# Seven-product pairs from feature tile 4 on: operands summed in place on VectorE, no negated operand, 57 activation slots

## The chip, the cores and the metric

The kernel runs on one core of one Trainium2 chip. The metric is device time of one launch in microseconds (us). TensorE (PE) does the matrix products, VectorE (DVE) and ScalarE (ACT) the elementwise work, GpSimd (POOL) a little elementwise work and the issue of those DMAs that add into their destination; SyncE (SP) issues the loads of weights.

## The reference

One step of a decoder trunk with one layer, in float32, for 520 tokens (512 prompt positions and 8 single-token samples), model width 1024, feed-forward width 3072:

```
x = x + W_o( sum_b sigmoid(g_b) * P_b(mixer_b(rmsnorm(x))) )    # pooling, RG-LRU and chunked gating branches
xn = rmsnorm(x, norm2_g)
g_pre = xn @ wg                                        # 1024 -> 3072
h = gelu(causal_conv3(prefix ++ g_pre)) * (xn @ wu)    # depthwise, width 3
x = x + h @ wd ;  y = rmsnorm(x, final_norm_g)
```

Beside `y`, the last rows of the inputs of each convolution, of the pooling window and of the recurrent state are returned. The change sits in the feed-forward part (`wg`, `wu`, `wd`) and in the loading of the old states and two small constants.

## The kernel before, in words

Activations lie transposed: features on the 128 partitions, the 520 tokens along the free axis, as two halves of 260. Every operand of a product is split into a high and a low part, and a product of a 128x128 weight tile with 520 tokens is three passes (high x high, high x low, low x high) over two halves, six matmuls of 260 columns (`mm`, line 202). A feature tile of `wg` or `wu` (m = 0 to 23) needs eight such k steps, 48 matmuls; this is the unit of time t in which the schedule counts.

**Order of the work.** The program has no scheduler behind it: each engine executes its instructions in the order in which the Python text issues them. `job` puts matrix products in a list; `run_jobs` (line 290) issues them and keeps a clock `now` that counts one unit per 48 matmuls. Work that belongs beside them is registered by `after(n, fn)` and `at(t, fn)` and issued when the clock passes that time (`run_later`, line 219); of equal times the one that was registered first goes first. So a step at t = 2.25 is placed behind everything that was issued before, on each engine, and an engine that waits for one instruction holds all later ones.

**Weights.** A `Chunk` is loaded by SP (`load`), rounded to its high part by ACT (`high`), and its low part is either a DVE subtraction (`low`, line 127) or, with `by_dma`, a negated copy on ACT and a DMA issued by POOL that adds the original weight from memory (`low_by_dma`, line 97). There are 4 raw, 6 high and 6 low buffers.

**Feed-forward.** After the eighth `w_o` product (t = 0 in this text) `g_post` and `fg_post` (lines 830, 936) take the `wg` products, `fg_rest` (842) does the convolution: one ACT pass (`tap0`), two DVE passes and a short one (`taps`), the gelu on ACT, and for m < 4 a DVE multiplication with the row factor of the norm (`scaled`). `u2_post` (951) multiplies with the `wu` product; `later_hilo` (964) splits the result for `wd`. The norm factor itself is computed by `rstd_small` (446) at the end of tile 0 and spread over the partitions by `rstd_bcast` (490) at the end of tile 1.

Tiles m = 0 to 3 use the unnormalized x times gain. Tiles 4 and 5 use normalized operands (`plain`, 897). From m = 6 on (`MP = 6`, line 1151) two feature tiles form a `Pair` (133): both tiles, as a 2x2 block matrix by k halves and tile, against the activations as a 2x2 block matrix by k halves and token halves, are computed with seven block products instead of eight (`PRODUCTS`, 143), 84 matmuls instead of 96. Sums of weight blocks are made by `sums` (172), split by `high` and `low`. The activation side needs seven operands X0 to X6, each as high and low part, made once by `operands` (915) from normalized blocks b (`rows`, 874), with DVE sums (`diff`) and splits (`operand`, 880). `run_pair` (244) issues a pair in the order of `SEQ_PAIR` (1150), 2.75 units long, with two `wd` products as fillers between the seven products:

```
SEQ_PAIR = (0, (0, 0), 3, 2, (0, 1), 1, 4, 5, (1, 0), 6, (1, 1))
```

Product 0 takes the weight operand h1, product 3 h2, product 2 h3; the low part of h3 is issued a quarter unit after the pair's start (`steps`, 189). X0 is a negated copy of X8, made on POOL (`minus_first`, 907). All activations come from one group of `NA = 51` equal slots (`A`, line 63).

Of the kernel before, what the change touches and what calls it, by code (L numbers as in the profile page):

```python
# [16 lines left out]
P = 128  # L17
# [34 lines left out]
def trunk_kernel(ctx: ExitStack, tc: tile.TileContext, t: dict, o: dict):  # L52
# [35 lines left out]
    sts = const.tile([P, NSTATE], F32, name="sts")  # L88
    wsT = const.tile([P, 4, P], F32, name="wsT")
    bsb = const.tile([P, 4, P], F32, name="bsb")  # L90
# [11 lines left out]
    class Chunk:  # L102
# [30 lines left out]
    class Pair:  # L133
# [29 lines left out]
        def low1(self):  # L163
            v.tensor_sub(self.new("h1", "wl"), self.raw[1], f(self.W["h1", "wh"]))  # L164
# [125 lines left out]
    def run_jobs():  # L290
# [3 lines left out]
        for n, e in enumerate(jobs):  # L294
            if e is None:
# [3 lines left out]
                for dt, fn in ((-2.25, c.load), (-0.75, c.high), (-0.5, c.low)):  # L299
                    at(t1 + dt, fn)  # L300
# [83 lines left out]
    def constants():  # L384
        nc.sync.dma_start(sts, t["sts"])
        nc.sync.dma_start(wsT, t["wsT"])
        nc.sync.dma_start(bsb.rearrange("p g i -> p (g i)"), t["bs"].partition_broadcast(P))
# [248 lines left out]
    def pool_post(gi, ps):  # L636
# [9 lines left out]
        def sums():  # L646
            g.tensor_copy(views["pool"][:, gi, :], a[:, SEQ:])
            v.tensor_reduce(st, pls[:, gi, :, 16 - w:], axis=mybir.AxisListType.X, op=ALU.add)
# [100 lines left out]
    def vmix(k):  # L749
        ps = PS1("vm")  # L750
        for c in range(4):
            te.matmul(ps[:, c * P:(c + 1) * P], vtok[c][:, k * P:(k + 1) * P], wsT[:, k, :], start=True, stop=True)  # L752
        m = A(f"mix{k}")
        v.tensor_tensor(m[:, :SEQ].rearrange("p (c i) -> p c i", c=4), ps.rearrange("p (c i) -> p c i", c=4),
                        bsb[:, k:k + 1, :].to_broadcast([P, 4, P]), op=ALU.add)
# [59 lines left out]
    def wo_post(j, ps):  # L815
# [3 lines left out]
        st2[0] = square_add(st2[0], x1[j], f"x1q{j}")  # L819

# [9 lines left out]
    def fg_post(m, ps):  # L830
# [5 lines left out]
        if m < MN:  # L836
            v.tensor_mul(two(ext[:, 2:]), acc(ps), two(rs2[0]))
        else:
            s.activation(two(ext[:, 2:]), acc(ps), AF.Copy)
        fg_rest(m, ext)  # L840

    def fg_rest(m, ext):
        y = A(f"fc{m}")

        def tap0():
            v.tensor_copy(views["ff"][:, m, :], ext[:, SEQ:])
# [9 lines left out]
        def scaled():  # L856
            if m < MN:
# [12 lines left out]
    def half_rows(q):  # L870
        i, h = q
        bq[q] = [A(f"b{i}{h}_{n}") for n in range(2)]

# [6 lines left out]
    def operand(n, xs):  # L880
        xo[n] = [(A(f"X{n}{i}h", F32R), A(f"X{n}{i}l", F32R)) for i in range(2)]
        for x, (h, _) in zip(xs, xo[n]):
            s.activation(h, x, AF.Copy)

        def lows():
            for x, (h, l) in zip(xs, xo[n]):
                v.tensor_sub(l, x, f(h))

        after(0.3, lows)
# [7 lines left out]
    def plain(k):  # L897

        return [[two(xo[n][k % 4 // 2][e])[:, k % 2, :] for n in ((8, 7), (1, 5))[k // 4]] for e in range(2)]

    def diff(n, a, b):
        y = [A(f"d{n}{i}") for i in range(2)]
        for i in range(2):
            v.tensor_sub(y[i], a[i], b[i])
        return y

    def minus_first(i):
        hl = [A(f"X0{i}_{e}", F32R) for e in "hl"]
        for q, p in zip(hl, xo[8][i]):
            g.tensor_scalar(q, f(p), -1.0, None, op0=ALU.mult)  # L910
        xo.setdefault(0, []).append(hl)

    dd = {}
# [336 lines left out]
```

## Time and profile before

| | |
|---|---|
| time, median of 3 runs | 870.24 us (870.08 to 870.30) |
| the profiled execution | 870.54 us, of which the span of the trace is 868.5 us |
| PE busy | 857.8 us (99%) in 7144 matmuls |
| DVE busy | 590.5 us (68%) |
| ACT busy | 443.4 us (51%) |
| POOL busy | 128.9 us (15%) |
| PE's time waiting for others | 3.8 us, in five waits |

The span runs from the first to the last instruction; 2.04 us of the execution lie around it. An engine's busy time counts overlapped work once. The start of an instruction minus the start of the one before it on the same engine is what one costs in an unbroken sequence; it is shorter than the duration given, since consecutive instructions overlap a little.

### The profile page before, as it was taken

The page shows a single profiled execution, that of the slowest core. Times are in us where ns is not written, and L with a number is a line of the kernel's source. Part 1 is how long each engine was busy: PE and PEld are TensorE (multiplying, and loading weights), DVE is VectorE, ACT ScalarE, POOL GpSimd, SP SyncE. Part 2 cuts the span into 40 slices and gives each one's busy share as a digit, 9 for nine tenths or more (in the row PEclk, how much of TensorE's full clock was granted, in tenths as well). Part 3 has the DMA queues.
Part 4 walks back from the last instruction along what each step waited for, and adds up shares of the span by engine and source line. Part 5 has one row for each costly group of instructions (what it writes and reads, how often), then busy time and mean ns, then how long its engine had stood idle before and what let it go on. Part 6 is the DMA issues. An engine that isn't in the chain of part 4 may idle for free.

```text
span 868.5 us, 16891 instructions
## 1 busy us (share of the span) xinstructions
PE 857.8 (99%) x7144; PEld 853.7 (98%) x7144; DVE 590.5 (68%) x920; ACT 443.4 (51%) x649; POOL 128.9 (15%) x185
## 2 busy tenths in 40 slices
PE   9999999999999999999999999999999999999996
PEld 7999999999999999999999999999999999999995
DVE  5897989698774443235554787677777767768655
ACT  6655465478342343222336675556556556556542
POOL 0502411111100000020002114111111110111143
PEclk9999999999999999999999999999999999999997
DMA  8433233222223233343345975655546555555642
GB/s 281 140 116 121 67 106 91 73 93 87 84 80 116 73 98 122 98 150 96 118 137 161 217 159 120 159 125 130 151 110 158 130 110 154 134 127 151 148 102 99
DMA packets 36251, 108.40 MB, mean 125 GB/s; under 512 B 4152, under 2 KB 7352, under 8 KB 36152
## 3 DMA queue, kind: packets, MB, share of 16 engines
q1 hardware_dynamic: 25440, 83.08, 30.4%
q0 software_dynamic: 9216, 22.68, 14.0%
q10 hardware_dynamic: 1520, 1.57, 0.5%
q8 instruction: 56, 0.92, 0.5%
q14 instruction: 19, 0.16, 0.1%
HBM read 92.13 MB, written 15.57 MB: 124 GB/s over the span
## 4 chain that ended last, share of the span: by engine, by line
PE 97%; DVE 1%; DMA 1%; ACT 0%; issue 0%; POOL 0%; DVEq 0%; POOLq 0%; ACTq 0%
PE pj L206 73%; PE pa L257 12%; PE c L257 6%; PE pf L257 3%; PE lru L206 1%; DMA x<-in_x 1%; PE vm L752 0%; DMA par<-in_par 0%; PE po L206 0%; DVE bc L522 0%; DVE y L1069 0%; PE vt L745 0%; ACT L540 0%; PE n30p L452 0%; PE n31p L452 0%
## 5 line engine op out<-in xcount | busy, mean ns | idle before, releaser
L127 DVE TENSOR_TENSOR wl<-raw,wh 128x1024 fp32r<-128x1024 f32 (+1 forms) x108 | 126.3, 1175 | 36.6 <-ACT wh L118 36.5
L206 PE MATMUL pj<-xn_h,wh 128*128 128x260 f32 x704 | 141.9, 283 | 0.1
L206 PE MATMUL pj<-xn_l,wh 128*128 128x260 f32 x704 | 141.4, 282 | 0.0
L206 PE MATMUL pj<-xn_h,wl 128*128 128x260 f32 x704 | 140.8, 281 | 0.0
L118 ACT ACTIVATE wh<-raw 128x1024 fp32r<-128x1024 f32 (+1 forms) x118 | 117.8, 1005 | 5.6 <-DMA raw<-in_w_in 3.5
L206 PEld LDWEIGHTS pj<-xn_l,wh 128*128 128x128 f32 x704 | 108.6, 188 | 0.0
L206 PEld LDWEIGHTS pj<-xn_h,wh 128*128 128x128 f32 x704 | 108.1, 188 | 0.3 <-ACT r L540 0.3
L206 PEld LDWEIGHTS pj<-xn_h,wl 128*128 128x128 f32 x704 | 108.2, 188 | 0.0
L206 PE MATMUL pj<-h_h,wh 128*128 128x260 f32 x384 | 82.4, 282 | 0.0
L206 PE MATMUL pj<-h_l,wh 128*128 128x260 f32 x384 | 82.4, 282 | 0.0
L206 PE MATMUL pj<-h_h,wl 128*128 128x260 f32 x384 | 82.3, 282 | 0.0
L1026 POOL DMA_DIRECT2D x1d<-dn x40 | 35.0, 875 | 264.0 <-ACT dn L1025 264.0
L206 PEld LDWEIGHTS pj<-h_l,wh 128*128 128x128 f32 x384 | 61.3, 188 | 0.0
L206 PEld LDWEIGHTS pj<-h_h,wl 128*128 128x128 f32 x384 | 61.2, 188 | 0.0
L206 PEld LDWEIGHTS pj<-h_h,wh 128*128 128x128 f32 x384 | 61.1, 188 | 0.0
L693 ACT ACTIVATE gt<-pj 128x520 f32<-128x520 f32 x24 | 14.5, 605 | 81.3 <-PE pj L206 81.2
L187 DVE TENSOR_TENSOR wl<-sum,wh 128x1024 fp32r<-128x1024 f32 x36 | 43.9, 1219 | 0.9 <-ACT wh L184 0.9
L164 DVE TENSOR_TENSOR wl<-raw,wh 128x1024 fp32r<-128x1024 f32 x18 | 22.0, 1224 | 31.9 <-ACT wh L161 31.9
L184 ACT ACTIVATE wh<-sum 128x1024 fp32r<-128x1024 f32 x36 | 37.8, 1050 | 0.8 <-DVE sum L179 0.8
L851 DVE SCALAR_TENSOR_TENSOR fc<-fg,par,fc 128x512 f32<-128x512 f32 x48 | 35.9, 749 | 1.2 <-ACT fc L847 0.3
L1025 ACT ACTIVATE dn<-pj 128x520 f32<-128x520 f32 x40 | 23.9, 597 | 6.4 <-PE pj L206 4.7
L206 PE MATMUL pj<-xg_l,wh 128*128 128x260 f32 x128 | 26.3, 287 | 0.3 <-DVE xg_l L1138 0.3
(488 smaller groups left out, 2320.5 us busy)
## 6 DMA issues: line engine op xcount, KB each, us to landing
raw<-in_w_in SPq DMA_DIRECT2D x50, 512.0 KB, 3.6
raw<-in_wg SPq DMA_DIRECT2D x24, 512.0 KB, 3.8
raw<-in_wu SPq DMA_DIRECT2D x24, 512.0 KB, 3.9
raw<-in_wd SPq DMA_DIRECT2D x24, 512.0 KB, 5.3
x1d<-dn POOLq DMA_DIRECT2D x40, 260.0 KB, 4.4
raw<-in_w_pb SPq DMA_DIRECT2D x8, 512.0 KB, 3.5
raw<-in_w_o SPq DMA_DIRECT2D x8, 512.0 KB, 3.6
wl<-in_wu POOLq DMA_DIRECT2D x6, 512.0 KB, 7.6
```

The lines of the kernel that those rows point to most:

```text
L118: s.activation(self.h[:, q], self.raw[:, q], AF.Copy)
L127: v.tensor_sub(self.l[:, q], self.raw[:, q], f(self.h[:, q]))
L164: v.tensor_sub(self.new("h1", "wl"), self.raw[1], f(self.W["h1", "wh"]))
L184: s.activation(self.new(n, "wh"), self.s[n], AF.Copy)
L187: v.tensor_sub(self.new(n, "wl"), self.s[n], f(self.W[n, "wh"]))
L206: te.matmul(ps[:, h, :TH], ww, xx[h] if isinstance(xx, list) else xx[:, h * TH:(h + 1) * TH], start=first and n == 0, stop=last and n == 2)
L257: te.matmul(bank[b], ww, xx, start=seen[b] + j + e == 0, stop=i >= (6, 1, 5)[b] and j == 3 and e == 2, skip_group_check=True)
L693: s.activation(two(y), acc(ps), AF.Sigmoid)
L851: v.scalar_tensor_tensor(y[:, :SEQ], ext[:, r:r + SEQ], pc("fcw", r * MF + m), y[:, :SEQ], op0=ALU.mult, op1=ALU.add)
L1025: s.activation(two(y), acc(ps), AF.Copy)
L1026: nc.gpsimd.dma_start(x1d[:, j, :], y, accum_op=ALU.add)
```

## The change

- `MP` goes from 6 to 4: tiles 4 and 5 of `wg` and of `wu` are pairs too; the jobs with `plain` operands and the operands X7 and X8 are gone.
- The norm factor is computed 0.75 unit after the last `w_o` product and spread at 1.5 (`N2`), no longer at the ends of tiles 0 and 1.
- The operands follow in a chain (`in_turn`): eight `rows` a quarter unit apart, then eleven steps 0.375 unit apart, in the order X0, X3, X1, X5, X2, X4, X6. The low parts of one step are issued at the start of the next. Three of the four differences overwrite their own input. X2 gets the opposite sign, X0 is no longer negated, and the sums that put a tile together use it with other signs (`add_parts`).
- Low parts of the `wg` chunks 0 and 1, of h1 in the two new pairs and of the first two `wd` chunks go from DVE to ACT and DMA.
- The copy of a tile's last columns to the output buffer (`views["ff"]`) goes from DVE to ACT, 24 times.
- `NA` goes from 51 to 57; the old states, two constants, the raw buffers of small weights and the warm-up operand move from own memory into these slots, and the states are loaded by four DMAs instead of one.

```
@@ Chunk, Pair
-                self.raw = wp.tile([P, self.size], F32, name="raw" + self.tag, bufs=2 if self.tag else RAW)
+                self.raw = A("rawq", w=self.size) if self.tag else wp.tile([P, self.size], F32, name="raw", bufs=RAW)
...
         def low1(self):
+            if self.by_dma:
+                low_by_dma(self.new("h1", "wl"), self.W["h1", "wh"], self.src[1])
+                return
             v.tensor_sub(self.new("h1", "wl"), self.raw[1], f(self.W["h1", "wh"]))
...
-            return ((-15, self.load), (-8, lambda: self.sums(0)), (-7, lambda: self.sums(1)), (-7, self.high1),
-                    (-6, lambda: self.sums(2)), (-6, self.low1), (-6, self.high0), (-5, self.low0),
+            return ((-15, self.load), (-8, lambda: self.sums(0)), (-7, lambda: self.sums(1)), (-11 if self.by_dma else -7, self.high1),
+                    (-6, lambda: self.sums(2)), (-10 if self.by_dma else -6, self.low1), (-6, self.high0), (-5, self.low0),
                     (-4, lambda: self.high("h2")), (-3, lambda: self.low("h2")), (-2, lambda: self.high("h3")),
                     (1, lambda: self.low("h3")))
@@ run_jobs
-                for dt, fn in ((-2.25, c.load), (-0.75, c.high), (-0.5, c.low)):
+                for dt, fn in zip((-3.25, -2.5, -2.25) if c.by_dma else (-2.25, -0.75, -0.5), (c.load, c.high, c.low)):
@@ constants
-        nc.sync.dma_start(sts, t["sts"])
-        nc.sync.dma_start(wsT, t["wsT"])
...
+        for d, c in ((h0t, S_H), (rcs, S_RC), (ffs, S_FF), (pls, S_PL)):
+            nc.sync.dma_start(d, t["sts"][:, c:c + d.shape[1]])
@@ wo_post
         st2[0] = square_add(st2[0], x1[j], f"x1q{j}")
+        if j == 7:
+            after(N2[0], norm2)
+            after(N2[1], norm2_rows)
@@ fg_post, fg_rest
-        if m < MN:
-            v.tensor_mul(two(ext[:, 2:]), acc(ps), two(rs2[0]))
-        else:
-            s.activation(two(ext[:, 2:]), acc(ps), AF.Copy)
+        v.tensor_mul(two(ext[:, 2:]), acc(ps), two(rs2[0]))
         fg_rest(m, ext)
...
-            v.tensor_copy(views["ff"][:, m, :], ext[:, SEQ:])
+            s.activation(views["ff"][:, m, :], ext[:, SEQ:], AF.Copy)
@@ operand, operands
-        after(0.3, lows)
+                if sign < 0:
+                    v.scalar_tensor_tensor(l, x, sign, f(h), op0=ALU.mult, op1=ALU.subtract)
+                else:
+                    v.tensor_sub(l, x, f(h))
+
+        pending.append(lows)
+
+    def in_turn(steps, dts):
+
+        while pending:
+            pending.pop(0)()
+        if steps:
+            steps[0]()
+            after(dts[0], lambda: in_turn(steps[1:], dts[1:]))
...
+    def onto(fn, o_, a, b):
+        for i in range(2):
+            fn(o_[i], a[i], b[i])
...
+        steps += [lambda: operand(0, b11), first_diff, lambda: operand(3, d3),
+                  lambda: onto(v.tensor_sub, b12, b22, b12), lambda: operand(1, b21),
+                  lambda: onto(v.tensor_add, d3, d3, b22), lambda: operand(5, b22), lambda: operand(2, d3, -1.0),
+                  lambda: onto(v.tensor_sub, d3, d3, b21), lambda: operand(4, b12), lambda: operand(6, d3)]
+        in_turn(steps, [XSTEP[0]] * 8 + [XSTEP[1]] * (len(steps) - 8))
@@ norm2, add_parts
+    def norm2():
+        n2[0] = rstd_small([st2[0]], D, "n2")
+
+    def norm2_rows():
+        rs2[0] = rstd_bcast(n2[0], "n2")
+        for i in range(8):
+            if i in held:
+                x = held.pop(i)
                 v.tensor_mul(x[:, 2:], x[:, 2:], rs2[0])
                 fg_rest(i, x)
+        after(0.25, operands)
...
+    def add_parts(n, o_, a, b):
+        if n == "c12":
+            v.scalar_tensor_tensor(o_, a, -1.0, b, op0=ALU.mult, op1=ALU.subtract)
+        else:
+            v.tensor_add(o_, a, b)
@@ wd_parts, mixer
+            wdc[p, j // 2] = Chunk(t["wd"][p, j // 2], KW, 2, timed=True, by_dma=p == 0 and j < 4)
...
+            pair_job(Pair(src[m], src[m + 1], m == MP), XP, out(m),
...
+            job([(Chunk(src[i], KD, timed=True, by_dma=True), 0, lambda k: xg2[k])],
@@ sizes
-NA, RAW, HS, LS, LOADS, HLEAD, LLEAD = 51, 4, 6, 6, 3, 3, 2
+NA, RAW, HS, LS, LOADS, HLEAD, LLEAD = 57, 4, 6, 6, 3, 3, 2
-MN, MP = 4, 6
-XSTEP = (0.4, 0.4)
+MP = 4
+N2 = (0.75, 1.5)
+XSTEP = (0.25, 0.375)
```

## Rows read from the trace of the kernel before

**Rows 1.** The page: the span, and busy time, share and instructions of each engine.

```profile
span 868.5 us, 16891 instructions
PE 857.8 (99%) x7144; PEld 853.7 (98%) x7144; DVE 590.5 (68%) x920; ACT 443.4 (51%) x649; POOL 128.9 (15%) x185
```

**Rows 2.** What PE waited for, longest first: line waited for, us in total, times, longest.

```profile
PE warm L1125 <- DVE wz L1122: 1.5, 1, 1.5
PE n30b L487 <- ACT n30d L461: 1.4, 1, 1.4
...
PE pj L206 <- ACT wh L118: 0.2, 1, 0.2
```

**Rows 3.** Busy time (and instructions) of PE, PEld, DVE, ACT and POOL in stretches of the span, then PE's granted clock, the DMA share and GB/s: ten microseconds near the start, and then the stretches that the text uses.

```profile
20.00:30.00 10.00, 10.00 (x86) 10.00 (x85) 6.84 (x9) 8.54 (x14) 7.61 (x10) 1.00 0.51 179
...
476.60:513.30 36.70, 36.70 (x309) 36.70 (x309) 28.42 (x58) 26.33 (x36) 5.37 (x9) 1.00 0.85 194
...
579.40:595.20 15.80, 15.80 (x135) 15.80 (x134) 11.47 (x18) 9.35 (x15) 1.87 (x4) 1.00 0.56 134
```

**Rows 4.** PE: from the chain that ended last, one product of a pair (start, us, what); then from the timeline of PE the first matmuls of tile 0 (466.01), the sums for the norm (n2p), the first matmuls of tile 1, the spreading of the norm factor (n2b), the first of `wu` tile 0, and the first of the first pair.

```profile
558.06 1.44 PE c L257 x12
...
466.01 0.41 PE L206 MATMUL pj<-x_h,wh 128*128 128x260 f32 x2
...
471.76 0.99 PE L452 MATMUL n2p<-ones,x1q 128*104 128x1 f32 x10
472.61 0.48 PE L206 MATMUL pj<-x_h,wh 128*128 128x260 f32 x2
...
478.46 0.65 PE L487 MATMUL n2b<-n2d,onesr 104*128 104x260 f32 x4
478.94 0.28 PE L206 MATMUL pj<-x_h,wh 128*128 128x260 f32 x1
...
547.84 0.28 PE L257 MATMUL pa<-X_h,wh 128*128 128x260 f32 x1
```

**Rows 5.** The timeline of DVE in unbroken sequences (start, us, line, operation, out<-in, count): where the next row follows at once, the difference of the starts is what one costs.

```profile
484.48 0.22 DVE L853 SCALAR_TENSOR_TENSOR fc<-fg,par,fst 128x8 f32<-128x8 f32 x1
484.61 1.68 DVE L878 SCALAR_TENSOR_TENSOR b<-xr,par,n2r 128x260 f32<-128x260 f32 x4
486.26 1.31 DVE L858 TENSOR_TENSOR fc<-fc,n2r 128x520 f32<-128x520 f32 x2
...
502.26 0.70 DVE L887 TENSOR_TENSOR X80l<-b,X80h 128x520 fp32r<-128x520 f32 x1
502.87 0.69 DVE L887 TENSOR_TENSOR X81l<-b,X81h 128x520 fp32r<-128x520 f32 x1
...
505.51 1.53 DVE L851 SCALAR_TENSOR_TENSOR fc<-fg,par,fc 128x512 f32<-128x512 f32 x2
506.96 0.22 DVE L853 SCALAR_TENSOR_TENSOR fc<-fg,par,fst 128x8 f32<-128x8 f32 x1
...
537.17 0.68 DVE L176 TENSOR_TENSOR sum<-raw 128x512 f32<-128x512 f32 x1
...
539.70 1.22 DVE L164 TENSOR_TENSOR wl<-raw,wh 128x1024 fp32r<-128x1024 f32 x1
...
542.91 1.22 DVE L187 TENSOR_TENSOR wl<-sum,wh 128x1024 fp32r<-128x1024 f32 x1
544.05 1.22 DVE L127 TENSOR_TENSOR wl<-raw,wh 128x1024 fp32r<-128x1024 f32 x1
```

**Rows 6.** The timeline of DVE: the last step of the norm factor, the first use of it, a wait for a gelu (in brackets the idle time before and what ended it), and the last low part of the operands.

```profile
475.90 0.70 DVE L465 TENSOR_TENSOR n2d<-ident,n2l 104x520 fp32r<-104x520 f32 x1
479.79 0.70 DVE L944 TENSOR_TENSOR fg<-fg,n2r 128x520 f32<-128x520 f32 x1 [3.18 <-ACT n2r L492]
...
501.64 0.70 DVE L858 TENSOR_TENSOR fc<-fc,n2r 128x520 f32<-128x520 f32 x1 [1.95 <-ACT fc L862]
...
526.90 1.11 DVE L887 TENSOR_TENSOR X61l<-d,X61h 128x520 fp32r<-128x520 f32 x1
```

**Rows 7.** The timeline of ACT: the table load for the square root, the copy of the norm factor, the convolution's first pass of two tiles, a weight's high part, the table load for the gelu and two gelus.

```profile
472.58 1.28 ACT L469 ACT_TABLE_LOAD   x1
...
479.16 0.60 ACT L492 ACTIVATE n2r<-n2b 128x520 f32<-128x520 f32 x1
480.58 1.65 ACT L847 ACTIVATE fc<-fg,par 128x512 f32<-128x512 f32 x2 [0.83 <-DVE fg L944]
482.14 1.04 ACT L118 ACTIVATE wh<-raw 128x1024 fp32r<-128x1024 f32 x1
...
484.30 1.28 ACT L862 ACT_TABLE_LOAD   x1
485.59 1.17 ACT L862 ACTIVATE fc<-fc 128x520 f32<-128x520 f32 x2
```

**Rows 8.** DMA issues between 466 and 556 us: what, queue, count, KB each, median us from issue to landing.

```profile
wl<-in_wu POOLq DMA_DIRECT2D x6, 512.0 KB, 7.6
```

**Rows 9.** The end of the kernel: two stretches of one microsecond, in the columns of rows 3, and two matmuls of 260 columns from PE's timeline.

```profile
859.00:860.00 1.00, 0.00 (x0) 0.00 (x0) 0.72 (x4) 0.73 (x3) 0.40 (x1) 0.85 0.00 0
860.00:861.00 1.00, 0.74 (x2) 0.47 (x3) 0.69 (x3) 0.00 (x0) 0.00 (x0) 0.50 0.00 0
...
861.20 0.64 PE L487 MATMUL n30c<-n30d,onesr 65*128 65x260 f32 x2
```

More of the change, by code (lines that the diff above doesn't have):

```diff
@@ L87, in trunk_kernel @@
     nc.scalar.dma_start(par, t["par"])
-    sts = const.tile([P, NSTATE], F32, name="sts")
-    wsT = const.tile([P, 4, P], F32, name="wsT")
-    bsb = const.tile([P, 4, P], F32, name="bsb")
+    h0t = const.tile([P, S_RC - S_H], F32, name="h0t")
+    early = {}
     def pc(n, i=0, m=1):
@@ L647, in sums @@
             g.tensor_copy(views["pool"][:, gi, :], a[:, SEQ:])
-            v.tensor_reduce(st, pls[:, gi, :, 16 - w:], axis=mybir.AxisListType.X, op=ALU.add)
+            v.tensor_reduce(st, early["pls"][:, gi, :, 16 - w:], axis=mybir.AxisListType.X, op=ALU.add)
             cur, k = a, 1
@@ L751, in vmix @@
         for c in range(4):
-            te.matmul(ps[:, c * P:(c + 1) * P], vtok[c][:, k * P:(k + 1) * P], wsT[:, k, :], start=True, stop=True)
+            te.matmul(ps[:, c * P:(c + 1) * P], vtok[c][:, k * P:(k + 1) * P], early["wsT"][:, k, :], start=True, stop=True)
         m = A(f"mix{k}")
         v.tensor_tensor(m[:, :SEQ].rearrange("p (c i) -> p c i", c=4), ps.rearrange("p (c i) -> p c i", c=4),
-                        bsb[:, k:k + 1, :].to_broadcast([P, 4, P]), op=ALU.add)
+                        early["bsb"][:, k:k + 1, :].to_broadcast([P, 4, P]), op=ALU.add)
         v.tensor_scalar(m[:, SEQ:], vt[k][:, SEQ:], pc("ws0", k), pc("bs0", k), op0=ALU.mult, op1=ALU.add)
@@ L895, in op_of @@
         return get
[L897 to L902, printed above, removed]
+    def onto(fn, o_, a, b):
         for i in range(2):
[L904 to L911, printed above, removed]
@@ new lines, in operands, with first_diff @@
+    def operands():
+        b11, b12, b21, b22 = (bq.setdefault(q, [A(f"b{q[0]}{q[1]}_{n}") for n in range(2)])
+                              for q in ((0, 0), (0, 1), (1, 0), (1, 1)))
+        d3 = []
+        def first_diff():
+            d3.extend(A(f"d{i}") for i in range(2))
+            onto(v.tensor_sub, d3, b11, b12)
+        steps = [lambda k=k: rows(k) for k in range(8)]
+        steps += [lambda: operand(0, b11), first_diff, lambda: operand(3, d3),
[3 more added lines that the diff above has]
+        in_turn(steps, [XSTEP[0]] * 8 + [XSTEP[1]] * (len(steps) - 8))
@@ L936, in g_post @@
     def g_post(m, ps):
         ext = fg_post(m, ps)
-        if m == 0:
-            held[0] = ext
-            n2[0] = rstd_small([st2[0]], D, "n2")
-        elif m == 1:
-            rs2[0] = rstd_bcast(n2[0], "n2")
-            for i, x in enumerate((held.pop(0), ext)):
+        if ext is not None:
+            held[m] = ext
+    def norm2():
[5 more added lines that the diff above has]
+                x = held.pop(i)
@@ L944, in g_post @@
                 v.tensor_mul(x[:, 2:], x[:, 2:], rs2[0])
                 fg_rest(i, x)
-            after(0.25, operands)
+        after(0.25, operands)
     n2 = [None]
@@ L1098, in mixer @@
         if m >= MP:
-            pair_job(Pair(src[m], src[m + 1]), XP, out(m),
+            pair_job(Pair(src[m], src[m + 1], m == MP), XP, out(m),
                      [(wd_parts(p, j), lambda ps, j=j: dn_post(p, j, ps, (0, 1))) for j in js])
@@ L1102, in mixer @@
         for i in (m, m + 1):
-            job([(Chunk(src[i], KD, timed=True, by_dma=post is u2_post or m >= 2), 0, plain if m >= MN else (lambda k: xg2[k]))],
+            job([(Chunk(src[i], KD, timed=True, by_dma=True), 0, lambda k: xg2[k])],
                 lambda ps, i=i: post(i, ps))
@@ L1120, in trunk_kernel @@
     s.activation(warm, ones, AF.Exp)
-    wz = const.tile([P, 512], BF16, name="wz")
+    wz = ap_.tile([P, 536], F32, name="wz", tag="a", bufs=NA)[:, :256].bitcast(BF16)
     v.memset(wz, 0.0)
```

55 lines of the change are left out of this document (20 added, 35 removed).

## The prediction

> **What bounds the kernel now.** I read the page first, then PE's waits, then the stretches, then the timelines of the engines around the place of the change. On the page the reader sees PE busy 857.8 of 868.5 us, and DVE, the next, only 590.5 [rows 1]. PE's waits are five and short, none between the first microseconds and the last sums [rows 2]; from 476.6 to 513.3 us it is busy 36.70 of 36.70 [rows 3]. So every matmul taken away shortens the kernel, as long as PE still never waits, and every wait that the change makes for PE is lost in full. The share of 68% for DVE is a mean: in that same stretch DVE is busy 28.42 of 36.70 us, in the later stretch of one pair (579.4 to 595.2) 11.47 of 15.80 [rows 3]. The new pairs begin at the end of the first of these.
>
> **PE's saving.** From the first matmul of `wu` tile 0 (478.94) to that of the first pair (547.84) lie 12 units, so a unit of 48 matmuls is 68.90 / 12 = 5.74 us, 0.120 us a matmul; 12 matmuls of a pair take 1.44, the same [rows 4]. Tiles 4 and 5 of `wg` and `wu` become two pairs: 2 x (96 - 84) = 24 matmuls less, **2.87 us**. The matmuls of the norm are only moved.
>
> **When the first pair now starts.** Tile 0 begins at 466.01. The norm's sums cost 472.61 - 466.01 - 5.74 = 0.86 us of PE, the spreading 478.94 - 472.61 - 5.74 = 0.59 [rows 4]. The first pair stands at t = 8: 466.01 + 8 x 5.74 + 1.45 = 513.4 us, instead of 547.84. That is 34.4 us earlier.
>
> **When the operands can start.** The sums are now issued at t = 0.75, at 470.3. Before, n2p began at 471.76 and the last step of the factor ended at 475.90 + 0.70 = 476.6, 4.84 us later, with the table load for the root in between [rows 4, 6, 7]. So it is ready at 475.2; the spreading at t = 1.5 is due at 475.5, and PE waits for nothing there (0.3 us to spare; if the spare is gone I lose 0.5 at most). DVE used the factor 1.33 us after n2b began (478.46 to 479.79) [rows 4, 6]: now at 476.8. That is 3.0 us earlier, against 34.4 us for the pair. Before, the last low part of the operands ended at 528.0 [rows 6], 19.8 us ahead of the pair; this spare time is less than what is taken.
>
> **What DVE must do ahead of the first pair.** PE goes through product 0, half a filler and product 3, and then needs for product 2 the low part of h3, which DVE gets issued last, at t = 8.25. PE is there at 513.4 + 3 x 1.44 = 517.7. In DVE's queue ahead of it stand, from 476.8 on, by the differences of starts in rows 5:
> - four tiles: 4 products with the factor (0.61 as for 502.26 to 502.87, from PSUM 0.70): 2.7; 4 times two convolution passes and the short one, (506.96 - 505.51) + 0.13 = 1.6: 6.4; 4 times `scaled` 0.61: 2.4; 4 products with `wu` 0.63: 2.5; 3 low parts 0.61: 1.8;
> - 16 rows of 260 columns, 1.65 / 4 = 0.41 each: 6.6;
> - 8 sums for the operands, 0.61: 4.9; 14 low parts, 0.61, X2's two as a form with a factor 0.67 (not among the rows in this size; 0.61 to 0.75 by its neighbours): 8.7;
> - the weights of the pair: four sums 539.70 - 537.17 = 2.5; low part of h0 0.6; low parts of h2 and h3, 1.14 each (542.91 to 544.05): 2.3.
>
> Together 41.5 us. Even with no idle time DVE ends at 476.8 + 41.5 = 518.3, already 0.6 us late. The four copies that go to ACT, the low parts of two `wg` chunks, of h1 and of the `wd` chunk are not in this sum; that is what the change gives back, and it isn't enough.
>
> **DVE's own waits.** It executes in order, and some entries wait for ACT:
> - the taps of tile 0 for ACT's copy and first pass after DVE's product: a pass is 1.65 / 2 = 0.82 or a little less [rows 7], the copy of ten columns on ACT is not in the trace, between DVE's shortest 0.13 [rows 5] and a whole pass 0.82; I take 0.2. Wait 1.1;
> - `scaled` of tile 0, issued at t = 2.25 ahead of tile 1's taps, for the gelu. ACT can begin tile 1's pass only when DVE has done its product at 481.6, behind taps and two rows; then copy 0.2, pass 0.8, a weight's high part 1.0, the table load 1.28, the gelu 0.55 [rows 7]: 485.5. DVE has run out at 482.4: wait 3.1. Before, taps and rows of both tiles stood ahead of the gelus; the trace shows such a wait at 501.64, 1.95 us [rows 6];
> - tile 2's taps as tile 0's, 1.1, and the low parts of X3 and X1, which wait for ACT's high parts made just before: 0.6 and 0.5.
>
> That is 6.4 us. h3's low part ends at 476.8 + 41.5 + 6.4 = 524.7 instead of 517.7: **PE waits 7.0 us** in all at the first pair, some 3.5 of it already ahead of product 3 for h2 (behind it still stand a low part of `wu` tile 2, X4, X6 and tile 3's product, which makes the rest). The first `wd` chunk's low part, by DMA with 7.6 us to landing [rows 8] from about 508.7, comes at 516.3 for a filler due at 514.8; that wait lies inside the 7.0. Adding up the order before in this way from 479.79 on ends X6 at 529.0, where the trace has 528.0 [rows 6], so my sum is somewhat long: I take 6.5, with 5.5 and 7.6 as its bounds by the bounds of ACT's copy and of ACT's order.
>
> **After it.** While PE waits, DVE and ACT work on. A pair needs 11.5 us of DVE in 15.8 [rows 3], in the two new ones 2.3 less for the low parts given to DMA; so the second pair finds h3 with 1.3 us to spare, and the rest is as before.
>
> **The other edits.** POOL's copies for X0 disappear; nobody waited for them. States and constants by six loads instead of three are issued where PE is busy 10.00 of 10.00 and the DMA share is 0.51 [rows 3]: weights are loaded some three units ahead, which hides them; nothing, at most 0.5. More slots: nothing gained, as no wait for a slot reaches PE [rows 2]. Copies on ACT in later pairs: 0.2 each beside an engine that is busy 9.35 of 15.80 [rows 3]: nothing.
>
> **The sum.** On the profiled execution 870.54 (span 868.5 and 2.04 around it): 870.54 - 2.87 + 6.5 = 874.2. It lay 0.30 over the median of the runs, 870.24; so the forecast is **873.9 us**, 0.4% slower.
>
> **Rivals.**
> - *DVE keeps up (faster).* If the queues fall so that DVE idles 2.3 us or less instead of 6.4, h3 is ready by 520.6 and PE loses less than the 2.87 it saves. With no idle at all: 870.24 - 2.87 + 0.6 = 868.0. For it: in this stretch DVE had 8.3 us of idle time before [rows 3], and the largest wait, 3.1, hangs on the place of one gelu behind a table load. Against it: the places follow from the order of issue. 12%.
> - *Half of it.* A wait of 1.1 to 4.6 us, about the saving: 868.5 to 872.0, middle 870.2. It needs that gelu wait to go and the others to stay. 15%.
> - *The clock falls.* PE stands still twice for about 3 us with 1.44 us of work between. [...] One or two products of 1.44 at half speed add 1.4 to 2.9: 875.3 to 876.8, middle 876.1. [...] 15%. [...]
> - *More than the first pair is late.* At t = 7.5 nearly all 57 slots are taken by X0 to X6, the old `xg2` and the tiles at work; if X6's slot is the one that X4's low parts just left, ACT waits for DVE, 1.2 us, and the second pair's 1.3 us are gone as well: 877. 8%.
>
> **How the numbers follow.** The forecast itself has 50%, its own range 872.7 to 875.0 (waits of 5.3 to 7.6). With the last two rivals slower has 0.73, the half way 0.15, faster 0.12; within 0.2%, 868.5 to 872.0, is about what a measurement can tell from no change. The range 868.6 to 877.2 leaves out the first rival and the far end of the last.
>
> **What would show it.** 7120 matmuls; a first pair at 513.4; PE waits at lines of the first pair, for the low parts of h2 and h3 on DVE, of 5.5 to 7.6 us in all, and DVE unbroken from 486 to 524 but for the small waits named. Wrong would be: h3's low part ready by 520; PE waiting at n2b; a clock under 1.00 between 514 and 530; waits in a later pair.

## The result and the profile after

The changed kernel takes **876.38 us** (median of 4 runs, 876.03 to 877.21) against 870.24: the ratio is 1.0072, 95% interval [1.0055, 1.009], so it is slower by 6.14 us. The forecast was 873.9, the range 868.6 to 877.2: right in direction and inside the range, but 2.5 us short. The time lies above the range of the forecast itself (872.7 to 875.0) and inside that of the rival in which the clock falls (875.3 to 876.8).

The page of the changed kernel, span and busy times (beside [rows 1]):

```profile
span 874.5 us, 16863 instructions
PE 859.3 (98%) x7120; PEld 854.5 (98%) x7120; DVE 594.0 (68%) x911; ACT 450.1 (51%) x683; POOL 124.1 (14%) x183
```

The matmuls fell from 7144 to 7120, and yet PE is busy longer, 859.3 instead of 857.8, in a span that is 6.0 longer. A busy PE that does less has worked more slowly; the waits alone can't tell that. They come next, longest first, in the columns of [rows 2]:

```profile
PE c L259 <- DVE wl L189: 2.0, 1, 2.0
PE warm L1133 <- DVE wz L1130: 1.5, 1, 1.5
PE n30b L494 <- ACT n30d L468: 1.4, 1, 1.4
PE pa L259 <- ACT m L263: 1.3, 1, 1.3
PE pa L259 <- DVE wl L189: 1.2, 1, 1.2
...
```

`warm` and `n30b` are the waits of before, at the two ends of the kernel; the four that are left out are of 0.4 us or less, at the ends too. Three are new, all at the first pair: product 3 (`c`) for the low part of h2, product 2 (`pa`) for ACT's copy at line 263, and product 2 again for the low part of h3. They make 4.5 us. On PE's timeline, with the idle time in brackets:

```profile
519.75 0.39 PE L259 MATMUL c<-X30h,wl 128*128 128x260 f32 x1 [1.97 <-DVE wl L189]
...
522.50 0.59 PE L259 MATMUL pa<-X20h,wh 128*128 128x260 f32 x1 [1.28 <-ACT m L263]
...
524.54 0.59 PE L259 MATMUL pa<-X20h,wl 128*128 128x260 f32 x1 [1.24 <-DVE wl L189]
```

The first matmul behind the first wait took 0.39 us, those behind the other two 0.59. The windows around them (columns as in [rows 3]; the number behind POOL's pair is PE's granted clock):

```profile
512.00:516.00 4.00, 4.00 (x36) 4.00 (x35) 4.00 (x8) 3.85 (x7) 0.00 (x0) 1.00 1.06 215
516.00:520.00 4.00, 2.03 (x17) 1.82 (x17) 4.00 (x7) 1.41 (x2) 0.00 (x0) 1.00 0.73 253
520.00:524.00 4.00, 2.02 (x12) 1.51 (x11) 4.00 (x7) 4.00 (x7) 0.31 (x1) 0.69 0.00 0
524.00:528.00 4.00, 3.46 (x16) 3.46 (x17) 3.55 (x6) 2.47 (x5) 1.42 (x2) 0.50 0.68 126
528.00:532.00 4.00, 4.00 (x33) 4.00 (x33) 1.16 (x3) 1.13 (x2) 1.02 (x3) 0.96 1.06 238
```

A full window holds 36 matmuls; these hold 17, 12 and 16. From 524 to 528 the granted clock is 0.50 although PE is busy for 3.46 of 4.00: the waits are followed by slow work. What that work costs stands in the chain that ended last (start, us, what):

```profile
524.54 2.54 PE pa L259 x10
527.08 2.07 PE pj L208 x12
529.15 1.44 PE pf L259 x12
```

Ten matmuls of product 2 took 2.54 where ten at full speed take 1.20, and the twelve of the filler 2.07 where twelve take 1.44: 1.34 + 0.63 = 2.0 us given to the clock. That is somewhat much, as the first matmul behind a wait is longer at full speed too (0.39 us in e4, at a granted clock of 1.00, where the next ones take 0.28): the same 22 matmuls take 4.45 here from start to start (524.54 to 528.99) and 2.74 in e4 below, where the clock stayed up (521.53 to 524.27), which makes it 1.7. From there on twelve matmuls take 1.44 again, and from 532 to 560 us the granted clock is 1.00.

Why the low part is late is read on DVE. The stretch from its first product with the norm factor to the end of h3's low part, in the columns of the windows above:

```profile
477.94:524.48 46.54, 42.11 (x345) 41.39 (x343) 41.00 (x72) 32.17 (x48) 5.34 (x8) 0.97 0.67 156
```

DVE (third pair of numbers) is busy 41.00 of 46.54 us. Its timeline, with the idle time before and what ended it in brackets, gives where the rest is (first the rows with the waits of 0.99 and more; the 1.59 ahead of the first row, for the norm factor, lies before the stretch) and then the two low parts at the end:

```profile
477.94 0.70 DVE L946 TENSOR_TENSOR fg<-fg,n2r 128x520 f32<-128x520 f32 x1 [1.59 <-ACT n2r L499]
479.63 1.54 DVE L858 SCALAR_TENSOR_TENSOR fc<-fg,par,fc 128x512 f32<-128x512 f32 x2 [0.99 <-ACT fc L854]
...
486.60 0.70 DVE L865 TENSOR_TENSOR fc<-fc,n2r 128x520 f32<-128x520 f32 x1 [3.09 <-ACT fc L869]
...
503.22 1.54 DVE L858 SCALAR_TENSOR_TENSOR fc<-fg,par,fc 128x512 f32<-128x512 f32 x2 [0.99 <-ACT fc L854]
...
518.48 1.21 DVE L189 TENSOR_TENSOR wl<-sum,wh 128x1024 fp32r<-128x1024 f32 x1
...
523.27 1.21 DVE L189 TENSOR_TENSOR wl<-sum,wh 128x1024 fp32r<-128x1024 f32 x1
```

The 3.09 is `scaled` of tile 0 waiting for a gelu. The first low part of the two ends at 519.69, the second at 524.48, and PE goes on at 519.75 and 524.54.

Last, the start of the first pair on PE's timeline:

```profile
514.50 0.28 PE L259 MATMUL pa<-X00h,wh 128*128 128x260 f32 x1
```

That is 1.1 later than the 513.4 of the prediction, and there is no wait of PE ahead of it but the short ones at the start, which were there before. The same shift stands at t = 0: the residual sum `xr` of the tile ahead of tile 0 begins on DVE at 467.26, where before it began at 466.21. So 1.05 us are lost before the first tile of `wg` has begun.

The account: -2.87 saved, +1.05 before t = 0, +5.5 up to h3's low part (PE was due at the third matmul of product 2, the first that wants it, at 514.50 + 3 x 1.44 + 0.24 = 519.06, and went on at 524.54), +2.0 for the clock: 5.7 (5.4 with 1.7 for the clock), where the span shows 6.0 and the runs 6.14. Of the rest, 0.35 lies far behind the first pair, where PE does not wait. From the first matmul of product 6 in one pair to that in the last pair stand the same 2112 matmuls, first in the kernel before, then in the changed one:

```profile
576.60 0.28 PE L257 MATMUL pa<-X60h,whq 128*128 128x260 f32 x1
...
829.73 0.28 PE L257 MATMUL pa<-X60h,whq 128*128 128x260 f32 x1
```

```profile
582.36 0.28 PE L259 MATMUL pa<-X60h,whq 128*128 128x260 f32 x1
...
835.84 0.28 PE L259 MATMUL pa<-X60h,whq 128*128 128x260 f32 x1
```

They take 253.13 us before and 253.48 after: 0.35 more, without a wait.

### The profile page after: what moved, and what is told of

Same layout as the page of the kernel before. It is cut to its first block, busy times and chain, and to the rows that moved or that the text cites. A ratio compares the mean times of both kernels' runs of the same rounds, so it can differ in the third digit from the quotient of the medians.

```text
span 874.5 us, 16863 instructions
## 1 busy us (share of the span) xinstructions
PE 859.3 (98%) x7120; PEld 854.5 (98%) x7120; DVE 594.0 (68%) x911; ACT 450.1 (51%) x683; POOL 124.1 (14%) x183
## 4 chain that ended last, share of the span: by engine, by line
PE 92%; DVE 5%; ACT 2%; issue 1%; DMA 1%; SPq 0%; POOL 0%; DVEq 0%; POOLq 0%; ACTq 0%
PE pj L208 66%; PE pa L259 13%; PE c L259 6%; PE pf L259 3%; PE lru L208 1%; DVE b L881 1%; DMA x<-in_x 1%; DVE fc L858 0%; PE vm L759 0%; PE po L208 0%; DVE fc L955 0%; DVE bc L529 0%; DVE y L1077 0%; DVE d L915 0%; DVE fg L846 0%
## 5 line engine op out<-in xcount | busy, mean ns | idle before, releaser
L126 DVE TENSOR_TENSOR wl<-raw,wh 128x1024 fp32r<-128x1024 f32 (+1 forms) x104 | 121.2, 1171 | 35.3 <-ACT wh L117 35.2
L117 ACT ACTIVATE wh<-raw 128x1024 fp32r<-128x1024 f32 (+1 forms) x114 | 113.6, 1003 | 4.3 <-DMA raw<-in_w_in 2.3
L189 DVE TENSOR_TENSOR wl<-sum,wh 128x1024 fp32r<-128x1024 f32 x40 | 48.7, 1217 | 0.0
L186 ACT ACTIVATE wh<-sum 128x1024 fp32r<-128x1024 f32 x40 | 42.0, 1050 | 0.0
L263 ACT ACTIVATE k<-c 128x260 f32<-128x260 f32 x20 | 7.7, 387 | 37.5 <-PE c L259 37.5
L263 ACT ACTIVATE m<-pa 128x260 f32<-128x260 f32 x40 | 15.3, 383 | 21.9 <-PE pa L259 21.8
```

The source lines that it names most:

```text
L117: s.activation(self.h[:, q], self.raw[:, q], AF.Copy)
L126: v.tensor_sub(self.l[:, q], self.raw[:, q], f(self.h[:, q]))
L186: s.activation(self.new(n, "wh"), self.s[n], AF.Copy)
L189: v.tensor_sub(self.new(n, "wl"), self.s[n], f(self.W[n, "wh"]))
L263: s.activation(kept["AFC"[b] + str(seen[b])], bank[b], AF.Copy)
```

## The experiments

Theory Q: DVE's queue ends too late, and that alone turns the saving into a loss. Theory C: about 2 us of it are the clock. Theory M: about 1 us comes from where the tiles now lie in memory. The rivals were that the new products themselves are dear, that the weights and not the queue are late, and that the clock is no loss because DVE is awaited anyhow.

**e1: the memory part alone, on the kernel before.** The loads of the states by four DMAs belong to it.

```
-    sts = const.tile([P, NSTATE], F32, name="sts")
+    h0t = const.tile([P, S_RC - S_H], F32, name="h0t")
...
-                self.raw = wp.tile([P, self.size], F32, name="raw" + self.tag, bufs=2 if self.tag else RAW)
+                self.raw = A("rawq", w=self.size) if self.tag else wp.tile([P, self.size], F32, name="raw", bufs=RAW)
...
-NA, RAW, HS, LS, LOADS, HLEAD, LLEAD = 51, 4, 6, 6, 3, 3, 2
+NA, RAW, HS, LS, LOADS, HLEAD, LLEAD = 57, 4, 6, 6, 3, 3, 2
```

> The kernel before with the memory part of the change alone: 57 slots, the states, two constants, the raw buffers of the small weights and the warm-up operand in them. In the changed kernel PE is 1.05 us late already at t = 0 (467.26 against 466.21 at the last product with x), without a wait. Theory M: the new places of the tiles in memory make PE's sequence a little slower (some 0.03 us a tile in places): 871.0 to 871.6 us, matmuls of 12 at 1.45 instead of 1.44. Rival: it comes from elsewhere in the change: 870.0 to 870.5. If slots had been a limit before, it would be faster, under 870.

871.41 us, ratio 1.0013 [1.0003, 1.0022]: 1.2 us slower, and PE has no new wait between its first 30 and its last 20 us (at the two ends two short ones came, of 0.2 and 0.3). The delay grows over the first 400 us and then no more: in the windows 20 to 100, 100 to 200, 200 to 300 and 300 to 400 e1 holds 2, 2, 1 and 4 matmuls less than the kernel before, from 400 to 460 one more. One row for each kernel shows it, from the windows (columns as in [rows 3]): a stretch of 344 us in which PE is idle for 0.1 us in all, first of the kernel before, then of e1.

```profile
30.00:374.00 344.00, 343.90 (x2884) 343.70 (x2885) 238.16 (x353) 163.59 (x216) 46.61 (x54) 1.00 0.31 95
```

```profile
30.00:374.00 344.00, 343.94 (x2874) 343.74 (x2874) 237.66 (x353) 163.60 (x216) 45.93 (x56) 1.00 0.31 97
```

Both are busy throughout at a clock of 1.00, but e1 got through ten matmuls less; at 343.9 / 2884 = 0.119 us each, that is 1.2 us (a count can be off by one at its edges, 0.12 us). The changed kernel got through 2873 there. So the memory part costs 1.2 us by the pace of the matmuls, and no wait shows it.

**e2: the change, with the new pairs from tile 6 on, as before.**

```
-MP = 4
+MP = 6
```

> The changed kernel with pairs from tile 6 on as before (tiles 4 and 5 with the unnormalized x); all other parts of the change stay. Main theory (what was lost is lost at the first new pair, waiting for DVE, and in the slow clock behind it): no wait of PE between 466 and 850, clock 1.00 throughout, 870.0 to 871.4 us, the upper end if the 1.05 us ahead of t = 0 stay. Rival (the moved norm, the copies on ACT or the low parts by DMA cost it): over 873.

872.26 us, ratio 1.0021 [1.0011, 1.003], 0.9 above the upper end of what was expected (871.4). Its waits are those of the kernel before: no wait in the middle of the kernel, 7144 matmuls, 2872 in the row of 344 us. So the sums in steps, the early norm and the copies on ACT bring no wait of PE; the new pairs in their early place do. Of its 2.0 us, 12 x 0.119 = 1.4 are the pace up to 374 us, and most of the rest is pace further on: the 2112 matmuls up to product 6 of the last pair take 253.64 (577.48 to 831.12), 0.5 more than before. In e1 they take 253.27 (578.28 to 831.55), only 0.14 more, so this later loss is not the memory part alone; its cause is open.

**e3: the first pair's weights h2 and h3 ahead of the operands.**

```
-                    (-4, lambda: self.high("h2")), (-3, lambda: self.low("h2")), (-2, lambda: self.high("h3")),
-                    (1, lambda: self.low("h3")))
+                    (-6 if self.first else -4, lambda: self.high("h2")), (-5 if self.first else -3, lambda: self.low("h2")),
+                    (-6 if self.first else -2, lambda: self.high("h3")), (-5 if self.first else 1, lambda: self.low("h3")))
```

> The changed kernel with the high and low parts of h2 and h3 of the first pair issued earlier (t = 6.5 to 6.75 instead of 7 to 8.25), ahead of X2, X4, X6 and of tile 3's product in DVE's queue. Theory Q (the whole queue is too long): h3's low part is ready some 6 us earlier, but the filler behind product 2 needs tile 3's low part of h, which stays where it was (525 us), and X2 is late by what h2 and h3 took; PE's wait moves there; 875 to 877 us. Rival P (only the place of h2 and h3 in the queue was wrong): the waits at products 3 and 2 go and nothing takes their place: 868 to 870.

876.15 us, ratio 1.0066 [1.005, 1.0083]: no gain that can be measured. The time is as expected, the place is not: a wait was expected at the filler behind product 2. The weights are there, and PE waits as long for something else; its waits and the row in its timeline:

```profile
PE pa L259 <- ACT m L263: 4.8, 1, 4.8
```

```profile
523.79 0.58 PE L259 MATMUL pa<-X20h,wh 128*128 128x260 f32 x1 [4.78 <-ACT m L263]
```

Product 2 goes into the bank of product 0, which ACT must have copied away. On ACT that copy stands behind `h_h` of a feature tile, and `h_h` waits for DVE:

```profile
520.83 0.64 ACT L968 ACTIVATE h_h<-fc 128x520 fp32r<-128x520 f32 x1 [3.83 <-DVE fc L955]
521.37 0.62 ACT L886 ACTIVATE X60h<-d 128x520 fp32r<-128x520 f32 x1
521.90 0.62 ACT L886 ACTIVATE X61h<-d 128x520 fp32r<-128x520 f32 x1
522.42 1.04 ACT L160 ACTIVATE wh<-raw 128x1024 fp32r<-128x1024 f32 x1
523.37 0.36 ACT L263 ACTIVATE m<-pa 128x260 f32<-128x260 f32 x1
```

The queue of DVE is late as a whole, and moving the entry that PE waits for only changes which later entry is waited for, here through a third engine. The wait of 1.28 for `m` in the changed kernel is the same link. The clock fell here too, behind a single wait:

```profile
520.00:524.00 4.00, 0.21 (x1) 0.21 (x2) 3.30 (x7) 3.17 (x6) 0.00 (x0) 0.67 0.00 0
524.00:528.00 4.00, 4.00 (x19) 4.00 (x20) 3.03 (x6) 3.65 (x6) 1.47 (x2) 0.50 0.36 48
```

PE was busy for the whole second window and got through 19 matmuls.

**e4: `scaled` of a feature tile half a unit later.**

```
-        after(0.75, scaled)
+        after(1.25, scaled)
```

> The changed kernel with the multiplication of tiles 0 to 3 with the norm factor issued half a unit later (1.25 instead of 0.75 after the tile's product), so that DVE doesn't stand before tile 0's gelu (idle 3.09 us at 486.60 in the changed kernel). Theory Q (DVE's queue is one chain up to h3): the idle time falls to under 0.5, all later steps come 2.6 to 3.1 us earlier, h3's low part ends near 521.6 instead of 524.4, PE waits 4 instead of 7 us: 873.2 with the slow clock as it was, 871.5 if the clock stays up. Rival (a later wait for ACT takes the time back): 875 to 876.5.

871.84 us, ratio 1.0021 [1.0011, 1.003]: 4.5 us of the 6.1 are back by one number. DVE's idle time of 3.09 ahead of `scaled` is gone, h3's low part ends at 521.48 instead of 524.48 (521.6 was expected), and PE has one wait in place of three:

```profile
521.53 0.39 PE L259 MATMUL pa<-X20h,wl 128*128 128x260 f32 x1 [2.14 <-DVE wl L189]
```

The windows of that wait and behind it:

```profile
516.00:520.00 4.00, 3.39 (x27) 3.04 (x25) 4.00 (x8) 4.00 (x7) 0.00 (x0) 1.00 0.07 30
520.00:524.00 4.00, 2.47 (x20) 2.47 (x21) 3.96 (x7) 2.86 (x5) 1.73 (x2) 1.00 0.56 102
524.00:528.00 4.00, 4.00 (x35) 4.00 (x34) 1.65 (x4) 1.77 (x4) 1.02 (x3) 1.00 1.03 234
```

PE stands still 0.61 us in the first and 1.53 in the second, and the granted clock is 1.00 here and in the other windows from 512 to 532 us. PE goes on with product 2 at 521.53 instead of 524.54, which is 3.0, and is not slowed behind it, which is 1.7: 4.7 by these rows as by the spans (874.5 and 869.8), 4.5 by the runs. 2.14 us of standing still did not bring the clock down; the 1.97 and 1.28 of the changed kernel, with ten matmuls between, did, and so did the 4.78 of e3.

**e6: spare matmuls in the place of the waits.** 16 ahead of product 3, 28 ahead of product 2, nothing else changed:

```
+            for _ in range(count):
+                te.matmul(bank[b], pair.W["h1", "wh"][:, :P], two(x)[:, 0, :], start=True, stop=True, skip_group_check=True)
...
+            if n == min(pairs) and x in (3, 2):
+                spare(*((2, 16) if x == 3 else (1, 28)))
```

> The change with 44 spare matmuls of 260 columns added in the first new pair, 16 ahead of product 3 and 28 ahead of product 2, into banks that are not in use yet; they compute nothing that is kept, and fill the time in which TensorE waits. The h3 low part still lands at about 524.5 us. Theory C (of what the change costs, about 2.0 us is the clock that fell because TensorE stood still twice): the granted clock stays 1.00 from 516 to 532 us, the weights' wait is as long as before, and the time is 876.4 - 2.0 = 874.4 us (874.0 to 875.0, with what the spare matmuls may reach beyond the waits). Rival (the clock would fall there anyway, or the slow stretch is no loss because VectorE is what is awaited): 876.0 or more, whether or not the clock stays up.

874.4 us (873.84 to 875.03), ratio 1.0045 [1.0031, 1.0059]. The windows of the place:

```profile
516.00:520.00 4.00, 3.93 (x33) 3.72 (x32) 4.00 (x6) 1.60 (x3) 0.00 (x0) 1.00 0.66 242
520.00:524.00 4.00, 4.00 (x36) 4.00 (x35) 4.00 (x7) 4.00 (x6) 0.49 (x1) 1.00 0.02 4
524.00:528.00 4.00, 4.00 (x35) 4.00 (x35) 3.50 (x6) 2.96 (x7) 1.24 (x2) 1.00 0.75 137
```

h3's low part is nearly as late as in the change (it begins at 523.08 instead of 523.27, and takes 1.22), and PE does 44 matmuls that nobody reads; the kernel is 2.0 us faster than the change. Product 1 begins at 527.09 instead of 528.99, 1.9 earlier, of which 0.2 was there at the start of the pair (514.30 instead of 514.50). That is theory C by itself: the slow clock was a loss on top of the wait, of 1.7 by these starts and 2.0 by the runs.

**e5: the order mended.** e3 and e4 together, and the last operand sums in the order in which products 3, 2 and 1 want them. Beside these, h1 of the other pair with low parts by DMA, and the chunk of its first filler, are rounded and completed a quarter unit later:

```
-                for dt, fn in zip((-3.25, -2.5, -2.25) if c.by_dma else (-2.25, -0.75, -0.5), (c.load, c.high, c.low)):
+                for dt, fn in zip(((-3.25, -2.5, -2.25) if pairs[n][0].first else (-3.25, -2.25, -2.0)) if c.by_dma else (-2.25, -0.75, -0.5), (c.load, c.high, c.low)):
...
-                   lambda: onto(v.tensor_sub, d3, d3, b21), lambda: operand(4, b12), lambda: operand(6, d3)]
-        in_turn(steps, [XSTEP[0]] * 8 + [XSTEP[1]] * (len(steps) - 8))
+                   lambda: operand(4, b12), lambda: onto(v.tensor_sub, d3, d3, b21), lambda: operand(6, d3)]
+        in_turn(steps, [XSTEP[0]] * 8 + [XSTEP[1]] * 8 + [1.875, 0.375, 0.375])
```

> The change with three moves in the order of its work and nothing taken out: `scaled` of a tile half a step later (as in e4), the first new pair's h2 and h3 high and low parts ahead of the operand sums (as in e3), and the last operand sums in the order in which products 3, 2 and 1 ask for them, so that ScalarE's copy of product 0's bank no longer stands behind a copy that waits for VectorE. Theory Q (the change is slower because VectorE's queue ends after TensorE asks for h3 low, and the saved matmuls are there to be had once it doesn't): no wait of TensorE over 0.5 us in the first pair, granted clock 1.00 from 512 to 532 us, and 870.24 - 2.87 of saved matmuls + 1.05 to 1.40 of the memory placement = 868.4 to 868.8 us; up to 0.5 more for a wait that is left. Rival (the new products themselves are dearer than the matmuls that they replace, wherever the queue stands): no wait in the first pair and still 870.5 or more. Rival (another engine takes over as the late one, as in e3): a wait of 2 us or more on ScalarE or VectorE in the first pair, and 871 or more.

**869.24 us** (868.8 to 869.74, 10 runs), ratio 0.9986 [0.9976, 0.9995]: faster than the kernel before by 1.0 us and than the change by 7.1. PE's waits have none in the middle of the kernel, the longest of those left is at an end:

```profile
PE warm L1133 <- DVE wz L1130: 1.5, 1, 1.5
PE n30b L494 <- ACT n30d L468: 1.4, 1, 1.4
PE n30p L459 <- POOL x2q L1053: 0.4, 1, 0.4
```

The clock is 1.00 from 512 to 532 us. The products are not dear, then; they were late. No run has the new order of the sums without the other moves, so what each adds to the 2.6 us that e5 gains over e4 is not shown. The time is 0.4 us over the upper end of what theory Q gave (868.8): 870.24 - 2.87 = 867.37, so 1.87 us are still missing. In the row of 344 us it got through 2873 matmuls, eleven less than before, which is 1.3 of them. The 2112 matmuls up to product 6 of the last pair take 253.58 (575.05 to 828.63), 0.45 more than before, which is most of the other 0.5.

**e7 to e11: where the tiles lie.** To ask what in the memory part slows the matmuls, a row of 32 bytes (64 in e11) is put ahead of all slots, and everything behind it lies that much further on; e10 changes the number of slots.

```
+    pad = ap_.tile([P, 8], F32, name="pad")
+    nc.gpsimd.memset(pad, 0.0)
     xT = [A(f"x{k}") for k in range(KD)]
```

e7 is e1 with the row:

> e1 (the kernel before with the memory part of the change alone) and one more 32-byte row ahead of all slots, so that every slot starts 32 bytes later in its partition; nothing else differs. The slots are 2144 bytes, an odd number of 32s, so with each slot the start relative to 64 bytes alternates; by the row of 57 slots the normed tiles stand the other way round from before, and the 32 bytes turn that back. Theory M64 (the +0.03 us in each tile of the products with the normed tiles comes from where these start relative to 64 bytes): the drift over the first 375 us is gone and the time is 870.0 to 870.6 us. Rival (it comes from something else in the memory part: the longer row, other neighbours, the A tiles): the drift stays, 871.2 to 871.6 us.

e8 is e5 with it:

> e5 with the same 32-byte row ahead of the slots. By theory Q with theory M64 the three terms that made the change slower are all gone and only the saved matmuls are left: 870.24 - 2.87 = 867.4 us (867.2 to 868.0), faster than both kernels. If Q holds and M64 does not: as e5, 868.4 to 868.8 us. If Q does not hold: 870 us or more.

e9 is the kernel before with it:

> The kernel before with one 32-byte row ahead of its 51 slots and nothing else changed. Theory P (where the tiles lie in the partition moves TensorE's pace by a few parts in a thousand of a per cent a matmul, and the placement of before happens to be a good one): slower than before by 0.5 to 1.5 us, 870.7 to 871.7, with no new wait of TensorE. Rival (a shift alone costs nothing to the kernel before; the cost of the memory part comes from its order of slots or from its longer row): 870.0 to 870.5.

e10 is e1 with `NA` of 56:

> e1 (the memory part of the change alone) with a row of 56 slots in place of 57. By the rival of e9 (order of slots): a slot less gives other tiles the same place, and the time moves away from e1's 871.4, to either side, by 0.4 us or more. By theory P too the time may be anywhere from 870.2 to 872.2. If it stays within 0.2 us of 871.4 the number of slots is not it, and the moved tiles (constants and raw loads put into slots) are.

e11 is e5 with a row of 64 bytes (`[P, 16]`):

> e5 with a row of 64 bytes ahead of the slots, where e8 had 32 (e8 was 0.7 us slower than e5). If the start relative to 64 bytes decides: as e5, 869.0 to 869.5 us. If any shift moves the time by some amount of its own: another value, 868 to 870.5 us, and the sum of terms for the memory placement stays a range and not a rule.

What was measured, with the matmuls of the row of 344 us. "Lost" is the time over 870.24 (870.39 in the runs of e9 to e11, the median of the kernel before beside them), for e5, e8 and e11 over that less 2.87; "by pace" is 0.119 us for each matmul under 2884.

| run | us | ratio to before | matmuls | by pace | lost |
|---|---|---|---|---|---|
| e9, before + 32 bytes | 871.04 | 1.0009 [1.0, 1.0018] | 2878 | 0.7 | 0.65 |
| e1, memory part | 871.41 | 1.0013 [1.0003, 1.0022] | 2874 | 1.2 | 1.2 |
| e10, 56 slots | 871.86 | 1.0018 [1.0009, 1.0027] | 2869 | 1.8 | 1.5 |
| e7, memory part + 32 bytes | 872.14 | 1.0019 [1.001, 1.0028] | 2869 | 1.8 | 1.9 |
| e5, mended order | 869.24 | 0.9986 [0.9976, 0.9995] | 2873 | 1.3 | 1.9 |
| e11, e5 + 64 bytes | 869.76 | 0.9994 [0.9985, 1.0003] | 2869 | 1.8 | 2.2 |
| e8, e5 + 32 bytes | 869.97 | 0.9993 [0.9984, 1.0002] | 2870 | 1.7 | 2.6 |

The row of e9 in the windows, whose only difference from before is the 32 bytes and the POOL instruction that clears them:

```profile
30.00:374.00 344.00, 343.93 (x2878) 343.72 (x2878) 237.49 (x352) 163.49 (x216) 44.91 (x53) 1.00 0.30 95
```

The theory that the start relative to 64 bytes decides has fallen: e7, in which the normed tiles start as before in that respect, is slower than e1 and not faster, above both values that were expected, and e11, shifted by a full 64 bytes, gets through 2869 matmuls where e5 has 2873. The theory that the order of slots or the length of the row is needed for it has fallen too, as e9 loses without either, though its interval only just reaches 1.0. e8 lies 1.2 us over what was expected of it without the 64-byte theory, and close to the 870 that was to speak against theory Q; but PE has no wait in the middle of e8 either, so what it lost is not lost in the queue. e10 is 1.5 over the kernel before where e1 is 1.2: the times do not tell 56 slots from 57. What is left is weaker: any shift tried moved the pace, always to the slow side of before, by 0.2% to 0.5% of the matmuls. The count itself repeats to one: the changed kernel and e2 to e6, which place their tiles alike, hold 2872 or 2873. Why the place matters has not been found. No run here tells the reads of the moving operand, those of the weights and the work of the other engines apart.

## Why the prediction was right, and where its sum fell short

- *The saving.* 24 matmuls less, 7120, and 2.87 us of them: e5 shows that they are to be had when PE does not wait.
- *The start of the first pair.* Predicted 513.4, measured 514.50. The step "nothing, at most 0.5" for **memory and more slots is the term that failed**: 1.05 us, by a slower pace from the start of the kernel, measured by itself as 1.2 in e1. I had looked for waits that the loads or the slots could bring [rows 2, 3], and there were none; that the place of the tiles could change the pace of the matmuls (2884 in 344 us before, 2878 in e9) was on no list of mine.
- *DVE's queue.* Forecast from 476.8: 41.5 us of work, 6.4 idle, 0.5 taken off, an end at 524.2. Measured from 477.94: 41.00 of work, 5.4 in waits, an end at 524.48. The start is later by the same 1.1 as the pair. That the end agrees to 0.3 us is partly luck: the start was 1.1 later, the queue 0.9 shorter. The waits were 0.99 (1.1 forecast), 3.09 (3.1), 0.99 (1.1), and 0.31 for a second `scaled` that I had not named; the low parts of X3 and X1 (0.6 and 0.5) waited for nothing. ACT's copy of ten columns, put at 0.2 between bounds of 0.13 and 0.82, takes 0.21. The 0.70 for a product with the factor from PSUM is its duration; what it costs by the starts in the changed kernel is 0.61 (482.02 to 482.63), as for the others, and X2's low parts cost 0.61 too (515.43 to 516.04) and not 0.67.
- *PE's wait.* Forecast 7.0, taken as 6.5 against a PE due at 517.7. Measured by the same reading 5.7, from 514.50 + 3 x 1.44 = 518.8 to 524.5. PE and DVE's queue both began 1.1 later, which cancels; the wait is shorter because the queue took 46.5 instead of 47.4. Predicted places: the low parts of h2 and h3. Both were there, but product 3 waited 1.97 and not some 3.5, and the filler ahead of it, for which a wait was forecast too, did not wait at all. The third place, ACT's copy of product 0's bank, was not named, and e3 shows that it alone would have held PE as long.
- *The clock.* It was a rival at 15%, priced at 1.4 to 2.9 us by half speed, the granted clock of 0.50 at the end of the kernel before [rows 9]; it came, for 1.7 to 2.0. **That it stood outside the sum is the second failure.** The two long waits were in the forecast itself, and the only rows with a granted clock under 1.00 [rows 9] had it at a wait of 1.4 us [rows 2], shorter than either of the two. By those rows it belonged in the main case, whose time is then the rival's own 876.1. In the trace of the changed kernel the clock was 0.69 and then 0.50 from the second wait on, but the matmuls behind the first wait of 1.97 ran at full speed (ten of them, 0.12 us apart, from 519.75), and in e4 a single wait of 2.14 left 1.00.
- *Its own signs.* One of the four signs that were to mean wrong came, a clock under 1.00 between 514 and 530; the other three did not.
- *What was to be nothing and was.* PE did not wait at n2b, no later pair waited, and POOL's copies, ACT's copies of ten columns and the loads of the states brought no wait of PE.

Two rivals were right in their condition though not for this kernel. "Half of it" asked for the wait at one gelu to go and the others to stay: e4 is that case, with 871.84 inside its 868.5 to 872.0. That DVE keeps up came with the order mended as well, in e5.

The sum with the measured terms: 870.24 - 2.87 + 1.05 + 5.5 + 2.0 = 875.9, and 0.35 of later pace make 876.3 (876.0 with 1.7 for the clock); measured 876.38. Two terms that were put at nothing, 1.05 and 2.0, stand against a wait that was put 1.0 too long. With the wait as forecast the time would have been some 877.4, above the range: that it lies inside is in part luck.

## To carry to other kernels

When work is pulled forward by tens of microseconds, sum the queue of the engine that prepares it, entry by entry with its own waits, to the time at which the bound engine asks; the length of the queue came out here as 46.5 us where 47.4 were forecast. A wait on the bound engine that is forecast at several microseconds, in one piece (4.78 us in e3) or in pieces with short work between (1.97 and 1.28 us around ten matmuls in the change), should carry the price of a slow clock, 1.7 to 2.0 us here, in the same line of the sum; the one wait of 2.14 us in e4 cost none. And when an operand is late, ask what else stands behind it in the same queue before moving it alone: in e3 the wait only changed its name, while moving the one entry that blocked the queue (e4) gave back 4.5 us of 6.1.

## What the runs showed of the hardware

- The pace of full-speed matmuls went with where the tiles lie: 2884 to 2869 matmuls in the same 344 us, at a granted clock of 1.00 and without a wait; 32 bytes ahead of all tiles cost 0.65 us (871.04 against 870.39, with an interval that just reaches no difference). The cause is open.
- Two waits of 1.97 and 1.28 us with ten matmuls between brought the granted clock to 0.69 and, behind a third of 1.24, to 0.50 (windows 520 to 524 and 524 to 528) and cost 1.7 to 2.0 us beyond the waits; so did one wait of 4.78 in e3 (0.67, then 0.50); one wait of 2.14 in e4 did not. Matmuls whose results nobody reads, put into the waits, gave the 2.0 us back (876.38 to 874.4).
